# Up projections of a two-layer encoder: two blocks of seven products per group in place of one, their sums folded into the group's own accumulators, and the convolution done in two halves

## The chip, the core and the metric

The kernel runs on one core of one Trainium2 chip. The metric is device time in microseconds (us) of one execution of the whole program; the kernel before takes 2402.25 us, the median of three runs (2401.57 to 2403.32).

## The reference, cut to what matters

Two encoder layers over 256 tokens of width 2048, all in float32. Each layer is an attention mixer with a residual, and a gated feed-forward net (FFN) with a residual. The change is in the FFN:

```python
def conv_ffn(x, w_up, conv_w, conv_b, w_down):
    h = jnp.einsum("bsd,df->bsf", x, w_up)          # 2048 -> 2 * 5632
    g, u = h[..., :D_FF], h[..., D_FF:]
    gp = jnp.pad(g, ((0, 0), (1, 1), (0, 0)))
    g = conv_w[0] * gp[:, :-2] + conv_w[1] * gp[:, 1:-1] + conv_w[2] * gp[:, 2:] + conv_b
    return jnp.einsum("bsf,fd->bsd", jax.nn.gelu(g) * u, w_down)
```

Its input `x` is the RMS-normalised residual stream. In the kernel the normalising factor of each token is applied behind the product (`rstd`), the gain before it.

## The kernel before, in words

**A product.** TensorE computes in a float32 form of reduced mantissa. Each float32 operand is therefore split into a high part (a cast on ScalarE, L231) and a low part (a subtraction on VectorE, L234), and each product is three matmuls into the same PSUM bank: high by high, high by low, low by high (L195 to L197). The activations of the FFN (`yT`, 16 tiles of 128 features by 256 tokens) are split once per layer. The weights are streamed: `wunit` loads 128 x 1024 float32 values (512 KB: two tiles of 128 rows by 512 columns) into `raw`, a ring of 5 buffers, by a DMA from the SyncE queue, casts them into `wh` and subtracts into `wl`, rings of 4 buffers each. `a_unit` then issues 12 matmuls of 128 x 512 with it: two tiles of 128 features by two blocks of 128 tokens by three. A unit's buffers come free when its last matmul is done, so ScalarE and VectorE can be at most some three units ahead of TensorE.

**The up projections.** `up_group` (L835) makes one of 11 groups per layer: 512 columns of the gate side (x=0) and 512 of the up side (x=1), each 8 units long, in the four PSUM banks of the tag `gm`, one for each side and token block. Four more banks, tags `s` and `tp`, serve everything else. Units 0 to 3 of both sides alternate, then come units 4 to 7 of the gate side and 4 to 7 of the up side.

**The block of seven products.** For unit 3 (`UPK`), the 2 x 2 x 2 block of token blocks, feature tiles and sides is done by the Strassen-Winograd scheme: seven products (21 matmuls) in place of eight (24), with sums of the activations formed once per layer (`y_forms`, L330) and sums of the weights formed by four subtractions of 128 x 512 on VectorE (L951 to L955) beside their splits (`column_forms`, L936). `seven_products` (L966) adds three of the products straight into three `gm` banks and puts four into the extra banks. `extra_parts` (L840) turns these into four sums in SBUF with a ScalarE copy and four VectorE additions, `scaled_parts` (L852) multiplies each by `rstd` on ScalarE, and at the end of a side VectorE reads the bank, multiplies by `rstd` and adds the sum (L878, two per side). The down projections use the same scheme, which the change leaves alone.

**Behind a side.** VectorE transposes the side in blocks of 32 x 32 (L279), and 16 small DMAs (L273, 12 from GpSimdE's queue, 4 from SyncE's) move the blocks into `qk` tiles, so that features lie on partitions. `convolved` (L889) works on the gate side: per 128 features one ScalarE operation and two on VectorE (L897, L899), then one Gelu over all. `multiplied` (L925) makes the product of the two sides (L928), sometimes the sums for the down projection (`row_forms`), and splits it.

**What sets the order.** Each engine runs its instructions in order. The builder's scheduler places them; the code postpones work with `later(n, fn)`, which runs `fn` at the n-th next `tick()`. `tick` stands in `up_group` after each of the units 0 to 3 and after every second unit of each side, eight per group. The convolution is due two ticks after the end of the gate side, the multiplication two after the end of the group. `ffn` (L1031) runs groups 0 to 5, the down projections of their features, groups 6 to 10, and theirs; a half's down projections are two calls of `chunk_pair` (L1017).

Of the kernel before, what the change touches and what calls it, by code (L numbers as in the profile page):

```python
# [71 lines left out]
def trunk_kernel(ctx: ExitStack, tc, a, out):  # L72
    nc = tc.nc
# [12 lines left out]
    def nm(s):  # L86
        uid[0] += 1
        return f"{s}_{uid[0]}"
# [27 lines left out]
    def tps(tag, bufs):  # L116
        return psum.tile([P, 512], F32, name=nm(tag), tag=tag, bufs=bufs)
# [179 lines left out]
    def transposes(c, gain, res):  # L297
# [4 lines left out]
        for j in range(4):  # L302
            res[c * 4 + j] = y_tile(ps[j // 2][:, j % 2, :], gain, c * 4 + j)

    def turned_rows(c, gain, res):

        z = att.tile([P, 2, 512], F32, name=nm("z"), tag="sc", bufs=1)
        V.transpose(z, h[:, :, c * 512:(c + 1) * 512])
        pf = att.tile([P, 8, P], F32, name=nm("hT"), tag="pt", bufs=2)
        moved(z.rearrange("p t k -> p (t k)"), pf)  # L310

        def tiles():
            for j in range(4):
                res[c * 4 + j] = y_tile(pf.rearrange("p (t j) q -> p j t q", t=2)[:, j], gain, c * 4 + j)
            if res is formed.get("of") and c == UPK // 2:
                y_forms(pf.rearrange("p (t j) q -> p j t q", t=2), gain)
        return tiles

    formed = {}
# [7 lines left out]
        V.tensor_tensor(f[:, 3], a12, f[:, 1], op=ALU.subtract)  # L327
        return f

    def y_forms(src, gain):  # L330

        y = tmp.tile([P, 2, 2, P], F32, name=nm("yf"), tag="ry")
        for k in range(2):
            S.activation(y[:, k], src[:, UPK % 2 * 2 + k], AF.Copy, scale=gain[:, 2 * UPK + k:2 * UPK + k + 1])
        f = form_sums("scc", *(y[:, k, t] for k in range(2) for t in range(2)))
        form = []
        for x, tag in enumerate(("R", "Rq")):
            high = tmp.tile([P, 2, P], F32R, name=nm("form"), tag="t0")
            low = const.tile([P, 2, P], F32R, name=nm("form"), tag=tag, bufs=1)
            split(high, low, f[:, 2 * x:2 * x + 2])  # L340
            form += [(high[:, k], low[:, k]) for k in range(2)]
        formed["form"] = form
# [71 lines left out]
    def quad(slot, dtype=F32):  # L414
        return att.tile([P, 4, SEQ], dtype, name=nm("qk"), tag=f"qk{slot}", bufs=1)
# [226 lines left out]
    def new_sc():  # L642
        return att.tile([P, 2, 512], F32, name=nm("sc"), tag="sc", bufs=1)
# [188 lines left out]
    yT = mixer_out(a["ev_out"], mix, ln[:, 2, :])  # L832


    def up_group(layer, j, yT, rstd, prod, *more):  # L835

        sides, extra, sums = {}, [], []
        src = [a["up"][layer, j, x] for x in range(2)]

        def extra_parts():  # L840

            b1, b5, b6, b7 = extra
            s1, x0, x1, y1 = (tmp.tile([P, 512], F32, name=nm("sum"), tag=tag) for tag in ("rx", "ry", "ry", "rx"))
            S.copy(s1, b1)
            V.tensor_tensor(x0, s1, b6, op=ALU.add)
            V.tensor_tensor(x1, x0, b7, op=ALU.add)
            V.tensor_tensor(x0, x0, b5, op=ALU.add)  # L847
            V.tensor_tensor(y1, x1, b5, op=ALU.add)
            sums.extend([[s1, x1], [x0, y1]])
            later(1, scaled_parts)  # L850

        def scaled_parts():  # L852

            for x in range(2):
                for t in range(2):
                    S.activation(sums[x][t], sums[x][t], AF.Copy, scale=rstd[0][:, t:t + 1])  # L856

        pss = [[tps("gm", 4), tps("gm", 4)] for _ in range(2)]
        for u in range(4):
            if not j and u == 2:  # L860
                rstd.append(row_factor())
            if u == UPK:
                extra += [tps("s", 2), tps("tp", 2), tps("tp", 2), tps("s", 2)]
                seven_products(pss, extra, column_forms(src, u, True), u, yT, formed["form"], True, True)
                later(1, extra_parts)
            else:
                for x in range(2):
                    a_unit(pss[x], src[x], u, yT, KT)
            tick()
        for x in range(2):  # L870
            for u in range(4, 8):
                a_unit(pss[x], src[x], u, yT, KT)
                if u % 2 == 1:
                    tick()
            z = (tmp.tile([P, 8, P], F32, name=nm("z"), tag="z", bufs=1) if x else
                 new_sc().rearrange("p t (f k) -> p (t f) k", k=P))
            for t in range(2):
                out = V.scalar_tensor_tensor(z.rearrange("p (f t) k -> p t f k", t=2)[:, t],  # L878
                                       pss[x][t].rearrange("p (f k) -> p f k", k=P), rstd[0][:, t:t + 1],
                                       sums[x][t].rearrange("p (f k) -> p f k", k=P), op0=ALU.mult, op1=ALU.add)  # L880
                if t:
                    tc.keep_in_program_order(out)
# [6 lines left out]
    def convolved(layer, j, sides):  # L889

        g4, c4 = sides[0], quad(4)
        sides[2] = c4
        for i in range(4):
# [3 lines left out]
            V.scalar_tensor_tensor(c[:, 1:SEQ], g[:, 0:SEQ - 1], convw[:, layer, 0, f:f + 1],  # L897
                                   c[:, 1:SEQ], op0=ALU.mult, op1=ALU.add)
            V.scalar_tensor_tensor(c[:, 0:SEQ - 1], g[:, 1:SEQ], convw[:, layer, 2, f:f + 1],  # L899
                                   c[:, 0:SEQ - 1], op0=ALU.mult, op1=ALU.add)  # L900
        S.activation(c4, c4, AF.Gelu_apprx_tanh)

    def new_forms(g0, n):

# [109 lines left out]
            tick()  # L1014
        return pss

    def chunk_pair(src, c, act, forms, nk, done):  # L1017

        nu = nk // 2
        heads = nu - 3 if nu > 10 else nu - 2  # L1020
        pss = pair_head(src, c, act, forms, sorted(forms), heads, nk)
        if not c:
            flush()
        for x in range(2):
            for u in range(heads, nu):
                a_unit(pss[x], src[c + x], u, act, nk)
            if c:
                tick()
            done(pss[x], c + x)

    def ffn(layer, yT, gain, last=False):  # L1031
        rstd, res = [], None
        for g0, g1, seven in HALVES:
            prod, forms = [], {}
            for j in range(g0, g1):
                up_group(layer, j, yT, rstd, prod, forms, g0, seven)
            nk = 4 * (g1 - g0)
            src = [a["down"][layer, c, 2 * g0:2 * g1] for c in range(4)]
            if g0:
                res = [None] * KT  # L1040
                if last:
                    finish_all(src, prod, forms, nk)
                    return
            for c in (0, 2):
                chunk_pair(src, c, prod, forms, nk, lambda ps, x: finish_chunk(ps, x, gain, res, 1 + x if x < 2 else 1))
        return res

    yT = ffn(0, yT, ln[:, 1, :])
# [280 lines left out]
def _paired_up(w):  # L1329

    w = w.copy()
    x, y = w[:, :, 0, UPK].copy(), w[:, :, 1, UPK].copy()
    w[:, :, 0, UPK] = np.concatenate([x[..., :512], y[..., :512]], axis=-1)
    w[:, :, 1, UPK] = np.concatenate([y[..., 512:], x[..., 512:]], axis=-1)
    return w


# [69 lines left out]
```

## Time and profile before

| | |
|---|---|
| runs | 2402.25 us (median of 3; 2401.57 to 2403.32) |
| the profiled execution | 2402.49 us, of which the span from first to last instruction is 2400.6 us |
| mean granted TensorE clock | 0.999 |
| matmuls, VectorE instructions, ScalarE instructions | 10895, 2461, 1954 |
| HBM read | 458.48 MB, 192 GB/s over the span |

Times in the profile are from the span's start. PE is TensorE, PEld its weight loads, DVE VectorE, ACT ScalarE, POOL GpSimdE, SP SyncE. The matmuls of the two FFNs' up projections lie from about 640 to 920 us, 1080 to 1325, 1690 to 1965 and 2110 to 2320 us. A matmul's shown duration overlaps that of the next one, since they are pipelined; how far apart two starts are tells what one costs. VectorE's and ScalarE's shown durations overlap a little too.

### The profile page before, as it was taken

What the parts mean: (1) busy time and instruction counts of PE and PEld (TensorE: products, weight loads), DVE (VectorE), ACT (ScalarE), POOL (GpSimd) and SP (SyncE); (2) the same over time, 40 slices, a digit from 0 to 9 for tenths busy, and PEclk for the clock granted to TensorE, in tenths of its full rate; (3) what the DMA queues carried; (4) which work ended last, traced back from release to release, by engine and by line L of the source; (5) the groups of instructions that cost most, each with busy time, mean ns of one, the idle gap of its engine ahead of it and who ended that gap; (6) DMA issues with size and microseconds to landing.
All of it is one profiled execution on the core that took longest, in us unless ns stands there. A gap on an engine that the chain in (4) does not pass through costs nothing.

```text
span 2400.6 us, 32954 instructions
## 1 busy us (share of the span) xinstructions
PE 2386.9 (99%) x10895; PEld 1983.1 (83%) x10895; DVE 1859.8 (77%) x2461; ACT 1374.5 (57%) x1954; POOL 539.7 (22%) x940
## 2 busy tenths in 40 slices
PE   9999999999999999999999999999999999999998
PEld 7888888888888888888888888888888888888887
DVE  6576567676778898778989867676788887788887
ACT  7455455566556565445656657555565654456664
POOL 1142023322222422004232100422223320033220
PEclk9999999999999999999999999999999999999999
DMA  8778678766767877668777764667678876678874
GB/s 306 208 196 236 198 198 237 211 201 193 215 198 220 222 216 212 204 206 216 213 227 211 220 204 134 188 202 206 208 215 222 217 220 199 207 218 213 241 212 156
DMA packets 287531, 505.64 MB, mean 211 GB/s; under 512 B 159096, under 2 KB 160504, under 8 KB 287360
## 3 DMA queue, kind: packets, MB, share of 16 engines
q1 hardware_dynamic: 256848, 470.15, 64.1%
q0 software_dynamic: 30080, 32.74, 8.0%
q8 instruction: 85, 1.39, 0.2%
q14 instruction: 86, 0.70, 0.1%
q10 hardware_dynamic: 432, 0.66, 0.1%
HBM read 458.48 MB, written 2.18 MB: 192 GB/s over the span
## 4 chain that ended last, share of the span: by engine, by line
PE 59%; DVE 3%; DMA 2%; issue 1%; POOL 1%; ACT 1%; SPq 1%; DVEq 0%; ACTq 0%; POOLq 0%
PE gm L196 16%; PE gm L197 16%; PE gm L195 16%; PE gm L145 2%; DVE wl L234 1%; PE gm L978 1%; PE gm L979 1%; PE gm L977 1%; POOL qk L273 1%; PE gm L150 1%; DMA qk<-z 1%; PE tp L978 1%; PE tp L979 1%; PE tp L977 1%; PE s L978 1%
## 5 line engine op out<-in xcount | busy, mean ns | idle before, releaser
L231 ACT CAST wh<-raw 128x1024 fp32r<-128x1024 f32 (+1 forms) x897 | 936.1, 1048 | 811.5 <-PE gm L197 607.3
L234 DVE TENSOR_TENSOR wl<-raw,wh 128x1024 fp32r<-128x1024 f32 (+1 forms) x897 | 1083.3, 1215 | 383.7 <-ACT wh L231 373.0
L196 PE MATMUL gm<-wl,yT 128*128 128x512 f32 x2092 | 815.6, 390 | 2.3 <-DVE wl L234 2.2
L195 PE MATMUL gm<-wh,yT 128*128 128x512 f32 x2092 | 816.1, 390 | 0.0
L197 PE MATMUL gm<-wh,yT 128*128 128x512 f32 x2092 | 814.6, 389 | 0.0
L196 PEld LDWEIGHTS gm<-wl,yT 128*128 128x128 f32 x2092 | 392.9, 188 | 86.2 <-DVE wl L234 6.3
L197 PEld LDWEIGHTS gm<-wh,yT 128*128 128x128 f32 x2092 | 392.8, 188 | 81.8 <-DVE yT L240 0.2
L195 PEld LDWEIGHTS gm<-wh,yT 128*128 128x128 f32 x2092 | 392.8, 188 | 81.2 <-issue 0.4
L273 POOL DMA_DIRECT2D qk<-sc x264 | 152.2, 584 | 855.3 <-issue 358.4
L273 POOL DMA_DIRECT2D qk<-z x392 | 226.3, 585 | 257.1 <-DVE z L279 232.7
L196 PE MATMUL gm<-wl,prod 128*128 128x512 f32 x518 | 201.5, 389 | 0.0
L195 PE MATMUL gm<-wh,prod 128*128 128x512 f32 x518 | 201.5, 389 | 0.0
L197 PE MATMUL gm<-wh,prod 128*128 128x512 f32 x518 | 201.5, 389 | 0.0
L196 PEld LDWEIGHTS gm<-wl,prod 128*128 128x128 f32 x518 | 97.3, 188 | 20.2
L195 PEld LDWEIGHTS gm<-wh,prod 128*128 128x128 f32 x518 | 97.2, 188 | 20.2
L197 PEld LDWEIGHTS gm<-wh,prod 128*128 128x128 f32 x518 | 97.2, 188 | 20.2
L196 PE MATMUL gm<-wl,mix 128*128 128x512 f32 x256 | 100.1, 391 | 0.4 <-DVE wl L234 0.4
L195 PE MATMUL gm<-wh,mix 128*128 128x512 f32 x256 | 100.0, 391 | 0.0
L197 PE MATMUL gm<-wh,mix 128*128 128x512 f32 x256 | 99.6, 390 | 0.0
L273 POOL DMA_DIRECT2D hT<-z x72 | 41.5, 585 | 199.6 <-PE gm L197 75.4
L856 ACT ACTIVATE sum<-sum,rstd 128x512 f32<-128x512 f32 x88 | 58.9, 716 | 25.4 <-DVE sum L847 16.1
L145 PE MATMUL gm<-yT,wh 128*128 128x512 f32 x256 | 59.5, 390 | 0.0
(356 smaller groups left out, 2640.0 us busy)
## 6 DMA issues: line engine op xcount, KB each, us to landing
raw<-in_up SPq DMA_DIRECT2D x352, 512.0 KB, 4.5
raw<-in_down SPq DMA_DIRECT2D x176, 512.0 KB, 4.4
raw<-in_eva_qk SPq DMA_DIRECT2D x96, 512.0 KB, 4.4
raw<-in_eva_v SPq DMA_DIRECT2D x46, 512.0 KB, 6.0
raw<-in_evb_qk SPq DMA_DIRECT2D x32, 512.0 KB, 4.6
raw<-in_ev_out SPq DMA_DIRECT2D x32, 512.0 KB, 4.3
raw<-in_od_qk SPq DMA_DIRECT2D x32, 512.0 KB, 4.1
raw<-in_od_out SPq DMA_DIRECT2D x32, 512.0 KB, 4.1
```

Of the source, the lines that this page charges most:

```text
L145: T.matmul(ps.rearrange("p a b -> p (a b)"), wh[:, k * P:(k + 1) * P], act[u * 8 + k].rearrange("p a b -> p (a b)"), start=(u == 0 and k = ...
L150: T.matmul(ps[:, 1, :], wl[:, k * P:(k + 1) * P], act[u * 8 + k][:, 0, :], start=False, stop=(u * 8 + k == KT - 1))
L195: T.matmul(ps[t], ah, wh[:, sl], start=(kt == 0), stop=False)
L196: T.matmul(ps[t], ah, wl[:, sl], start=False, stop=False)
L197: T.matmul(ps[t], al, wh[:, sl], start=False, stop=(kt == nk - 1))
L231: first = S.copy(dst_h, src)
L234: V.tensor_tensor(dst_l, src, dst_h.bitcast(F32), op=ALU.subtract)
L273: (nc.sync if i in on_sync else G).dma_start(dst[j * 32:(j + 1) * 32, :, i * 32:(i + 1) * 32], z[i * 32:(i + 1) * 32].rearrange("p (b j c) ...
L856: S.activation(sums[x][t], sums[x][t], AF.Copy, scale=rstd[0][:, t:t + 1])
L977: T.matmul(ps, ah, wh, start=own and first, stop=False)
L978: T.matmul(ps, ah, wl, start=False, stop=False)
L979: T.matmul(ps, al, wh, start=False, stop=own and last)
```

## The change

- **Which units.** `UPK` becomes `(1, 3)`: units 1 and 3 are done by seven products each, in every group but a layer's first, which is done in full. The host's packing of the weights (`_paired_up`) follows.
- **The front.** The four products of a block that went into the extra banks are issued ahead, while the group before is still running (`up_front`): those of unit 1 ahead of the third unit from the end of its gate side, those of unit 3 ahead of the third from the end of its up side. For group 6 they stand in the second `chunk_pair` of the down projections. Both units' products add up in the same four banks.
- **The fold.** `merged` forms the Winograd sums inside these four banks (ScalarE copies into two of them, VectorE additions into two), and the banks then *are* the next group's accumulators. The groups take the banks `gm` and `s`/`tp` by turns.
- **The direct products.** The three products left of each block (`up_direct`) are added on top when the group starts. They need the other side's weight unit as it is, which is loaded a second time for that, and split. The form `t4` made in the front is kept till then.
- **The order of units.** A group does all units of the gate side (0, 2, 4 to 7), then all of the up side, with six ticks.
- **The end of a side.** ScalarE reads each bank and multiplies by `rstd` (two per side); `sums`, `scaled_parts` and L878 go. Both sides use one buffer `z`.
- **The convolution** is due in two halves, two and four ticks behind the gate side, each with a Gelu of its own; the multiplication three ticks behind the group.

```diff
-UPK = 3
+UPK = (1, 3)
...
+    def up_front(layer, j, yT):
+        gm = (j >= HALVES[0][1]) == j % 2
+        b1, b7, b6, b5 = (tps(*(("gm", 4) if gm else (tag, 2))) for tag in ("s", "s", "tp", "tp"))
+        direct = []
+        def block(n):
+            u = UPK[n]
+            w11, t1, t2, t3, t4 = front_forms([a["up"][layer, j, x] for x in range(2)], u, j)
+            s1, s2, s3, s4 = formed[u]
+            for ps, form, w in ((b1, token_block(yT, 2 * u, 0), w11), (b7, s3, t3), (b6, s2, t2), (b5, s1, t1)):
+                products(ps, form, w, n == 0, u == UPK[-1])
+            direct.append((u, s4, t4))
+        def merged():
+            s1, x0, x1 = (tmp.tile([P, 512], F32, name=nm("sum"), tag=tag) for tag in ("rx", "ry", "ry"))
+            S.copy(s1, b1)
+            V.tensor_tensor(x0, s1, b6, op=ALU.add)
+            V.tensor_tensor(x1, x0, b7, op=ALU.add)
+            V.tensor_tensor(b6, x0, b5, op=ALU.add)
+            S.copy(b7, x1)
+            V.tensor_tensor(b5, x1, b5, op=ALU.add)
+        block(0)
+        return [[b1, b7], [b6, b5]], direct, merged, block
...
+    def front_forms(src, u, home):
+        ra, rb = (wts.tile([P, UN], F32, name=nm("raw"), tag="raw", bufs=RAW) for _ in range(2))
+        nc.sync.dma_start(ra, src[0][u])
+        nc.sync.dma_start(rb, src[1][u])
+        w11, w12, w22, w21 = ra[:, 0:512], ra[:, 512:UN], rb[:, 0:512], rb[:, 512:UN]
+        t1 = tmp.tile([P, 512], F32, name=nm("t1"), tag="rx")
+        V.tensor_tensor(t1, w12, w11, op=ALU.subtract)
+        V.tensor_tensor(w12, w22, w12, op=ALU.subtract)
+        wa, wb = ([wts.tile([P, UN], F32R, name=nm(x), tag=x, bufs=4) for x in ("wh", "wl")] for _ in range(2))
+        split(*wa, ra)
+        V.tensor_tensor(w22, w22, t1, op=ALU.subtract)
+        split(*(x[:, 0:512] for x in wb), w22)
+        split(*(x[:, 512:UN] for x in wb), t1)
+        V.tensor_tensor(w21, w21, w22, op=ALU.subtract)
+        t4 = fourth(home, u)
+        split(*t4, w21)
...
+    def up_direct(pss, src, yT, u, s4, t4):
+        wh, wl = wunit(src[1][u])
+        products(pss[1][0], s4, [x[:, 0:512] for x in (wh, wl)], onto=True)
+        products(pss[0][0], token_block(yT, 2 * u + 1, 0), [x[:, 512:UN] for x in (wh, wl)], onto=True)
+        products(pss[0][1], token_block(yT, 2 * u + 1, 1), t4, onto=True)
...
+        for x in range(2):
+            for n, u in enumerate(units):
+                if not x and u == units[-3] and after:
+                    nxt = up_front(*after)
+                if x and nxt and u == units[-3]:
+                    nxt[3](1)
...
+                    own_unit(pss[x], src[x], u, yT, u == units[-1])
...
+            if x and nxt:
+                nxt[2]()
+            z = new_z("f k")
             for t in range(2):
-                out = V.scalar_tensor_tensor(z.rearrange("p (f t) k -> p t f k", t=2)[:, t],
-                                       pss[x][t].rearrange("p (f k) -> p f k", k=P), rstd[0][:, t:t + 1],
-                                       sums[x][t].rearrange("p (f k) -> p f k", k=P), op0=ALU.mult, op1=ALU.add)
+                S.activation(z.rearrange("p (f t) k -> p t f k", t=2)[:, t],
+                             pss[x][t].rearrange("p (f k) -> p f k", k=P), AF.Copy, scale=rstd[0][:, t:t + 1])
...
-                later(2, lambda: convolved(layer, j, sides))
-        later(2, lambda: multiplied(j, sides, prod, *more))
+                later(2, lambda: convolved(layer, j, sides, 0))
+                later(4, lambda: convolved(layer, j, sides, 1))
+        later(3, lambda: multiplied(j, sides, prod, *more))
```

Over the whole program TensorE issues 54 matmuls of 128 x 512 fewer (18 blocks more, three spared by each), VectorE 64 instructions more, ScalarE 124 more, and SyncE 40 loads of 512 KB more; GpSimdE's count is the same.

**VectorE at a block's forms.** Before, in the second group of a half: `t` and `raw` are the weight sums (L951 to L955), `wl` and `form` the low parts, `qk` the convolution.

```order
L951 TENSOR_TENSOR t_3218_16883<-raw_16879 128x512
L234 TENSOR_TENSOR wl_16842<-raw_16839,wh_16841 128x1024
L897 SCALAR_TENSOR_TENSOR qk_16707<-qk_16617,convw,qk_16707 128x255 x2
L899 SCALAR_TENSOR_TENSOR qk_16707<-qk_16617,convw,qk_16707 128x255 x2
L897 SCALAR_TENSOR_TENSOR qk_16707<-qk_16617,convw,qk_16707 128x255 x2
L899 SCALAR_TENSOR_TENSOR qk_16707<-qk_16617,convw,qk_16707 128x255 x2
L234 TENSOR_TENSOR wl_16860<-raw_16857,wh_16859 128x1024
L952 TENSOR_TENSOR raw_16879<-raw_16880,raw_16879 128x512
L234 TENSOR_TENSOR wl_16887<-raw_16880,wh_16886 128x1024
L234 TENSOR_TENSOR form_16897<-t_3218_16883,form_16896 128x512
L954 TENSOR_TENSOR raw_16880<-raw_16880,t_3218_16883 128x512
L234 TENSOR_TENSOR wl_16893<-raw_16879,wh_16892 128x1024
```

Now, on the gate side of a group, for the block of unit 1 of the next one (the sums are L894 to L901):

```order
L279 STREAM_TRANSPOSE z_16480<-z_16480 128x1024
L234 TENSOR_TENSOR wl_16552<-raw_16549,wh_16551 128x1024
L974 SCALAR_TENSOR_TENSOR qk_16427<-qk_16302,convw,qk_16427 128x255 x2
L234 TENSOR_TENSOR wl_16577<-raw_16574,wh_16576 128x1024
L894 TENSOR_TENSOR t_3142_16600<-raw_16596 128x512
L895 TENSOR_TENSOR raw_16596<-raw_16597,raw_16596 128x512
L898 TENSOR_TENSOR raw_16597<-raw_16597,t_3142_16600 128x512
L901 TENSOR_TENSOR raw_16597<-raw_16597 128x512
L234 TENSOR_TENSOR wl_16604<-raw_16596,wh_16603 128x1024
L234 TENSOR_TENSOR wl_16606<-raw_16597,wh_16605 128x512
L234 TENSOR_TENSOR wl_16606<-t_3142_16600,wh_16605 128x512
L234 TENSOR_TENSOR form_16615<-raw_16597,form_16615 128x512
```

The convolution no longer stands between a block's forms (its last two operations come ahead of them), and the block has one split of 128 x 1024 and three of 128 x 512 where it had three and one.

**VectorE at the end of a group.** Before, the four sums (L845 to L848) and the end of the gate side:

```order
L845 TENSOR_TENSOR sum_16926<-sum_16925,tp_16877 128x512
L234 TENSOR_TENSOR wl_16977<-raw_16974,wh_16976 128x1024
L846 TENSOR_TENSOR sum_16927<-sum_16926,s_16878 128x512
L234 TENSOR_TENSOR wl_16995<-raw_16992,wh_16994 128x1024
L847 TENSOR_TENSOR sum_16926<-sum_16926,tp_16876 128x512
L848 TENSOR_TENSOR sum_16928<-sum_16927,tp_16876 128x512
L234 TENSOR_TENSOR wl_17034<-raw_17031,wh_17033 128x1024
L234 TENSOR_TENSOR wl_17052<-raw_17049,wh_17051 128x1024
L234 TENSOR_TENSOR wl_17070<-raw_17067,wh_17069 128x1024
L878 SCALAR_TENSOR_TENSOR sc_17010<-gm_16742,rstd_15653,sum_16925 128x4x128
L878 SCALAR_TENSOR_TENSOR sc_17010<-gm_16743,rstd_15653,sum_16927 128x4x128
L279 STREAM_TRANSPOSE sc_17010<-sc_17010 128x1024
```

Now, on the up side: the fold (L862 to L866), the splits of the next group's two direct units (`wl_16914`, `wl_16929`) and of its unit 0, six of the eight convolution operations (L972, L974), and the transpose:

```order
L862 TENSOR_TENSOR sum_16882<-sum_16881,tp_16594 128x512
L234 TENSOR_TENSOR wl_16866<-raw_16863,wh_16865 128x1024
L863 TENSOR_TENSOR sum_16883<-sum_16882,s_16593 128x512
L864 TENSOR_TENSOR tp_16594<-sum_16882,tp_16595 128x512
L866 TENSOR_TENSOR tp_16595<-sum_16883,tp_16595 128x512
L234 TENSOR_TENSOR wl_16914<-raw_16911,wh_16913 128x1024
L972 SCALAR_TENSOR_TENSOR qk_16837<-qk_16712,convw,qk_16837 128x255 x2
L974 SCALAR_TENSOR_TENSOR qk_16837<-qk_16712,convw,qk_16837 128x255 x2
L234 TENSOR_TENSOR wl_16929<-raw_16926,wh_16928 128x1024
L234 TENSOR_TENSOR wl_16944<-raw_16941,wh_16943 128x1024
L972 SCALAR_TENSOR_TENSOR qk_16837<-qk_16712,convw,qk_16837 128x255 x2
L279 STREAM_TRANSPOSE z_16890<-z_16890 128x1024
```

The fold stands around the split of the side's last unit (`wl_16866`) and ahead of all that the next group needs; three splits of the next group stand ahead of the transpose, which waits for the end of the side, as three of the up side's stood before.

**TensorE at the start of a group.** Before, the last product of a group is followed by unit 0 of the gate and of the up side, in `gm` banks. Now the accumulators `s_16592`, `s_16593` and `tp_16594` were made by the front, and the direct products go onto them:

```order
L877 MATMUL gm_16197<-wh_16865,yT_15709 128x512
L877 MATMUL tp_16594<-wh_16913,form_15395 128x512
L877 MATMUL tp_16594<-wl_16914,form_15395 128x512
L877 MATMUL tp_16594<-wh_16913,form_15396 128x512
L877 MATMUL s_16592<-wh_16913,yT_15380 128x512
L877 MATMUL s_16592<-wl_16914,yT_15380 128x512
L877 MATMUL s_16592<-wh_16913,yT_15380 128x512
L877 MATMUL s_16593<-form_16615,yT_15380 128x512 x3
L877 MATMUL tp_16594<-wh_16928,form_15455 128x512
L877 MATMUL tp_16594<-wl_16929,form_15455 128x512
```

So the first matmul of a group now waits for the third VectorE addition of the fold (L864), and the seventh for ScalarE's copy behind the second.

More of the change, by code (lines that the diff above doesn't have):

```diff
@@ L870, in up_group, with token_block, products @@
[L870 to L873, printed above, removed]
+            V.tensor_tensor(b6, x0, b5, op=ALU.add)
[3 more added lines that the diff above has]
+        return [[b1, b7], [b6, b5]], direct, merged, block
+    def token_block(act, kt, t):
+        return [act[kt][:, x, t * P:(t + 1) * P] for x in range(2)]
+    def products(ps, form, w, first=False, last=False, onto=False):
+        (ah, al), (wh, wl) = form, w
+        for i, (x, y) in enumerate(((ah, wh), (ah, wl), (al, wh))):
+            T.matmul(ps, x, y, start=first and i == 0, stop=last and i == 2, skip_group_check=onto)
@@ new lines, in own_unit @@
+    def own_unit(ps, src, u, act, last):
+        wh, wl = wunit(src[u])
+        for t, k in [(t, k) for t in range(2) for k in range(2)] if last else [(t, k) for k in range(2) for t in range(2)]:
+            sl = slice(k * 512, (k + 1) * 512)
+            products(ps[t], token_block(act, 2 * u + k, t), [x[:, sl] for x in (wh, wl)], last=last and k == 1, onto=True)
+    def up_direct(pss, src, yT, u, s4, t4):
[3 more added lines that the diff above has]
+        products(pss[0][1], token_block(yT, 2 * u + 1, 1), t4, onto=True)
@@ new lines, in up_group @@
+    def up_group(layer, j, yT, rstd, prod, front, after, *more):
+        sides = {}
+        src = [a["up"][layer, j, x] for x in range(2)]
+        if front:
+            pss, direct = front[:2]
+            units = [u for u in range(8) if u not in UPK]
+            for u, s4, t4 in direct:
+                up_direct(pss, src, yT, u, s4, t4)
+        else:
+            pss = [[tps("gm", 4), tps("gm", 4)] for _ in range(2)]
+            units = list(range(8))
+        nxt = None
+        for x in range(2):
+            for n, u in enumerate(units):
+                if not j and not x and u == 2:
+                    rstd.append(row_factor())
+                if not x and u == units[-3] and after:
+                    nxt = up_front(*after)
+                if x and nxt and u == units[-3]:
+                    nxt[3](1)
+                if front:
+                    own_unit(pss[x], src[x], u, yT, u == units[-1])
+                else:
+                    a_unit(pss[x], src[x], u, yT, KT)
+                if n % 2 == 1 or n == len(units) - 1 and n % 2 == 0:
@@ L1015, in pair_head, with chunk_pair @@
         return pss
-    def chunk_pair(src, c, act, forms, nk, done):
+    def chunk_pair(src, c, act, forms, nk, done, after=None):
         nu = nk // 2
+        nxt = None
         heads = nu - 3 if nu > 10 else nu - 2
@@ L1025, in chunk_pair @@
             for u in range(heads, nu):
+                if not x and u == nu - 1 and after:
+                    nxt = up_front(*after)
+                if x and nxt and u == nu - 2:
+                    nxt[3](1)
                 a_unit(pss[x], src[c + x], u, act, nk)
+            if x and nxt:
+                nxt[2]()
             if c:
@@ L1035, in ffn @@
             for j in range(g0, g1):
-                up_group(layer, j, yT, rstd, prod, forms, g0, seven)
+                front = up_group(layer, j, yT, rstd, prod, front, j + 1 < g1 and (layer, j + 1, yT), forms, g0, seven)
             nk = 4 * (g1 - g0)
@@ L1044, in ffn @@
             for c in (0, 2):
-                chunk_pair(src, c, prod, forms, nk, lambda ps, x: finish_chunk(ps, x, gain, res, 1 + x if x < 2 else 1))
+                front = chunk_pair(src, c, prod, forms, nk,
+                                   lambda ps, x: finish_chunk(ps, x, gain, res, 1 + x if x < 2 else 1),
+                                   c and not g0 and (layer, g1, yT))
         return res
```

85 lines of the change are left out of this document (39 added, 46 removed).

## The prediction

> **What bounds the kernel now.** I read the page first, then the busy times by stretch, then TensorE's waits, then the timeline of one group. The page gives the span and the engines:
>
> ```profile
> span 2400.6 us, 32954 instructions
> PE 2386.9 (99%) x10895; PEld 1983.1 (83%) x10895; DVE 1859.8 (77%) x2461; ACT 1374.5 (57%) x1954; POOL 539.7 (22%) x940
> ```
>
> TensorE is busy for all but 13.7 us. An average over stages may hide a stage with another limit, so here are three stretches by engine (columns: stretch, its length, then busy us and count of PE, PEld, DVE, ACT, POOL, the granted clock, the DMA engines' busy share, GB/s): one period of an up group in layer 1, 40 us of up groups in layer 0, and 40 us of down projections.
>
> ```profile
> 1832.38:1875.78 43.40, 43.20 (x190) 35.41 (x189) 38.07 (x52) 26.58 (x36) 13.83 (x24) 1.00 0.81 222
> 1160.00:1200.00 40.00, 40.00 (x178) 33.09 (x177) 34.30 (x47) 24.59 (x32) 13.82 (x24) 1.00 0.75 209
> 1000.00:1040.00 40.00, 40.00 (x178) 33.07 (x177) 32.30 (x35) 20.05 (x21) 0.00 (x0) 1.00 0.70 220
> ```
>
> In the up groups too TensorE is the limit, at full clock; VectorE is second with 38.07 of 43.40 us (88%), ScalarE has over a third to spare. What TensorE waited for in the FFNs (us in total, times, longest), with two rows of the waits of the others in layer 1:
>
> ```profile
> PE gm L196 <- DVE wl L234: 2.5, 5, 0.9
> PE tp L978 <- DVE wl L234: 0.6, 1, 0.6
> ...
> ACT wh L231 <- PE gm L197: 196.7, 133, 3.6
> ...
> DVE t L951 <- DMA raw<-in_up: 5.6, 8, 1.2
> ```
>
> So it waited 3.1 us in all, each time for VectorE's low parts. The third row says why it is so little: ScalarE's casts wait for TensorE to give a buffer back, that is, weights are ready up to three units ahead. The up groups' own stalls lie where the reserve runs out, behind the block of seven products:
>
> ```profile
> 1824.90 0.39 PE L195 MATMUL gm<-wh,yT 128*128 128x512 f32 x1
> ...
> 1832.38 0.39 PE L977 MATMUL gm<-wh,yT 128*128 128x512 f32 x1
> ...
> 1837.21 0.39 PE L195 MATMUL gm<-wh,yT 128*128 128x512 f32 x1
> 1837.80 0.50 PE L196 MATMUL gm<-wl,yT 128*128 128x512 f32 x1 [0.20 <-DVE wl L234]
> 1838.13 0.40 PE L197 MATMUL gm<-wh,yT 128*128 128x512 f32 x1
> ...
> 1875.78 0.39 PE L977 MATMUL gm<-wh,yT 128*128 128x512 f32 x1
> ```
>
> From 1824.90 to 1832.38 there are 33 matmuls: 7.48 / 33 = 0.2267 us each, whatever the 0.39 us shown. The block's 21 take 1837.21 - 1832.38 = 4.83 us, 0.07 more than 21 x 0.2267. Then come 0.59 and 0.33 us where 0.227 each is usual: a stall of 0.36 and 0.10 of restart, 0.46 in all. 189 matmuls make the period: 42.84 + 0.07 + 0.46 = 43.37, measured 43.40.
>
> **The change, term by term.** *Matmuls removed.* A block spares three. Before there are 22 blocks (two layers by 11 groups), after 40 (two layers by 10 groups by two); 18 x 3 = 54 matmuls go, and since TensorE is the limit each is worth its distance: 54 x 0.2267 = **-12.2 us**. [...]
>
> *Slower products.* The 18 blocks more bring the block's excess of 0.07 us with them, **+1.3 us**. Products on a bank that another engine wrote are not in the trace; the nearest rows are these same ones, so I bound the term by 0 and 2.6 us (twice the excess) and keep 1.3.
>
> *VectorE per group.* Its rows, with starts that tell what one costs when they follow each other:
>
> ```profile
> 1859.17 1.40 DVE L878 SCALAR_TENSOR_TENSOR z<-gm,rstd,sum 128x512 f32<-128x512 f32 x2
> 1860.61 1.25 DVE L279 STREAM_TRANSPOSE z<-z 128x1024 f32<-128x1024 f32 x1
> 1861.78 1.19 DVE L234 TENSOR_TENSOR wl<-raw,wh 128x1024 fp32r<-128x1024 f32 x1
> ...
> 1865.15 0.87 DVE L897 SCALAR_TENSOR_TENSOR qk<-qk,convw,qk 128x255 f32<-128x255 f32 x2
> 1865.94 0.87 DVE L899 SCALAR_TENSOR_TENSOR qk<-qk,convw,qk 128x255 f32<-128x255 f32 x2
> ...
> 1869.45 0.68 DVE L952 TENSOR_TENSOR raw<-raw,raw 128x512 f32<-128x512 f32 x1
> 1870.05 1.22 DVE L234 TENSOR_TENSOR wl<-raw,wh 128x1024 fp32r<-128x1024 f32 x1
> 1871.19 0.68 DVE L234 TENSOR_TENSOR form<-t,form 128x512 fp32r<-128x512 f32 x1
> 1871.79 0.68 DVE L954 TENSOR_TENSOR raw<-raw,t 128x512 f32<-128x512 f32 x1
> ```
>
> A 512-wide subtraction or low part takes 0.60 us (1869.45 to 1870.05), a 1024-wide one 1.14, the two L878 1.44, a transpose 1.17, two convolution steps 0.79. Plain units stay at 14 (12 own, 2 direct). The old block is four subtractions, three wide low parts and one narrow; the two new ones have eight, two and six: +4 x 0.60 - 1.14 + 5 x 0.60 = +4.26. The four sums stay four. The four L878 go: -2.88. Net +1.4 us on 38.07, 39.5 us, while TensorE's share is 186 x 0.2267 + 0.14 = 42.3 us. VectorE goes from 88% to 93% of the group and isn't the limit. What matters then is whether its work comes in time.
>
> *ScalarE* loses four scalings per group and gains four bank reads, one Gelu call, a copy, and the narrower casts. For the reads the nearest row is the scaling; for the casts, the rows by group:
>
> ```profile
> L856 ACT ACTIVATE sum<-sum,rstd 128x512 f32<-128x512 f32 x88 | 58.9, 716 | 25.4 <-DVE sum L847 16.1 <-DVE sum L845 8.8 <-ACT wh L231 0.2
> L231 ACT CAST form<-t 128x512 fp32r<-128x512 f32 x37 | 22.8, 615 | 3.8 <-DVE t L951 3.8
> ```
>
> Reads for scalings cancel; five narrow casts more, one wide cast less, a copy and a call come to about 3.5 us on 26.58, some 30 of 42.3. It is hidden.
>
> *Where the reserve gets lowest.* Take the order of the instructions and the times above. At the end of the gate side ScalarE reads two banks (2 x 0.72, taken as 1.4 us) and VectorE transposes (1.17), with three splits already done ahead, 36 matmuls or 8.2 us. The front of unit 3 comes after those 36. VectorE then has one subtraction (0.6; two were done) and a wide split (1.14): ready at 1.4 + 1.17 + 1.74 = 4.3 us, needed at 8.2. The fold: its last bank is filled at 8.2 + 2.7 = 10.9 us, four additions are 2.4 and the copies on ScalarE perhaps 1, done by 14.5 at the latest; the direct products need it at the side's end, 84 x 0.2267 = 19.0 us. Margin 4.5. Up to there VectorE has the transpose, 0.60 + 1.14 + 3 x 0.60 of the forms, three splits, the fold, three splits ahead and six convolution steps: 1.17 + 3.54 + 3.42 + 2.40 + 3.42 + 2.37 = 16.3, with 1.4 of waiting 17.7 of 19.0. On the gate side TensorE does 18 direct, 72 plain and 12 front matmuls, 23.1 us. The front of unit 1 comes behind 18 + 36 of them, at 12.2 us; VectorE reaches its first operand after 1.4 + 1.17 + 0.79 + 2 x 1.14 + 4 x 0.60 + 1.14 = 9.2. Margin 3.0, the lowest of all. So in a steady group I see no stall, and the 3.1 us that the old burst of VectorE costs (convolution, block, multiplication and sums in one go) go for the most part: **-2.5 us** (bounds 0 and -3.7, the waits with six restarts of 0.1).
>
> *New waits.* At each layer's start and in front of group 6 the front falls beside other bursts (row sums, `h` additions), which the trace doesn't show together. Taking the longest wait shown, 0.9, for about one of these places: **+1.0 us** (0 to 9.2, see the first rival). Loads of weights: 18 units per group in place of 16. From the third stretch, 0.70 x 40 us for 220 GB/s x 40 us / 0.524 MB = 16.8 units, a unit is 1.67 us of all the DMA engines; two more per group raise the share from about 0.78 to 0.87. A load takes
>
> ```profile
> raw<-in_up SPq DMA_DIRECT2D x352, 512.0 KB, 4.5
> ```
>
> 4.5 us, and five buffers at 42.3 / 18 = 2.35 us apart leave 11.7, less what VectorE is ahead. I take it as hidden. The small moves keep their number and their queues; SyncE's four per side stand ahead of loads as before.
>
> *Sum*, against the profiled execution's 2402.49 us (its span is 2400.6; the median of the runs is 0.24 lower): -12.2 + 1.3 - 2.5 + 1.0 = -12.4 us, which gives **2390 us**.
>
> **The rivals.** *One stall per group remains.* The reserve runs out once in each of the 20 groups, say at the front of unit 1, at the old price of 0.46 us: 20 x 0.46 = 9.2 us, which replaces the term of +1.0 and the -2.5. Then 2402.5 - 12.2 + 1.3 + 9.2 - 3.1 = 2398 us. For it: VectorE at 93%, and 5.6 us in eight waits of its first subtraction for a load. Against: the margin of 3.0 us. Chance 0.15.
>
> *VectorE becomes the limit (slower).* Its work may not overlap as I counted. The multiplication, its splits, and the row sums that half of the groups have, are four kinds of rows (mean ns, or lowest, median and highest):
>
> ```profile
> L928 DVE TENSOR_TENSOR qk<-qk,qk 128x1024 f32<-128x1024 f32 x22 | 26.9, 1221 | 2.0 <-issue 1.1 <-DMA qk<-z 0.7
> L234 DVE TENSOR_TENSOR prod<-qk,prod 128x256 fp32r<-128x256 f32 x88 | 32.6, 417 | 0.0
> L324 DVE TENSOR_TENSOR sums<-qk x12: 282/284/289, 765.5 to 2261.9; 128x128 f32<-128x128 f32 x12
> L234 DVE TENSOR_TENSOR form<-sums,form 128x512 fp32r<-128x512 f32 x8 | 5.5, 683 | 0.0
> ```
>
> They make 1.22 + 4 x 0.42 + 4 x 0.28 + 0.68 = 4.7 us. If each instruction kept its whole shown duration, a group would have 14 + 2 wide low parts at 1.22, eight subtractions, six narrow low parts and four sums at 0.68, two transposes at 1.25, eight convolution steps at 0.48 (0.87 less half of 0.79) and these 4.7: 19.5 + 12.2 + 2.5 + 3.8 + 4.7 = 42.7 us, and with one wait of 1.4 for the banks 44.1, against TensorE's 42.3. In 20 groups 1.8 us each: 2390 + 36 = 2426 us. It decides from the point where VectorE needs over 40.9 us per group. The rows above speak against it: a start follows 0.60 us after one that lasts 0.68. [...] Chance 0.06.
>
> *The loads become late (slower).* At a DMA share of 0.87 a load may wait in line; if each of the 40 fronts gets its two tiles so late that the margin of 3.0 us is used up and TensorE waits the 0.7 us (5.6 / 8) that VectorE's first subtraction waits now, that is 28 us: 2418 us. Against: a share of 0.81 in the first stretch, without a wait of TensorE's that names a load. Chance 0.05.
>
> *It doesn't spare the matmuls:* excluded, the new order has 54 fewer.
>
> **How the numbers follow.** A measurement of this kernel can tell about 0.2%, 4.8 us, from no change. The forecast, all stalls together under some 4 us, has 0.74 and lies wholly on the faster side; the first rival, 0.15, is spread about 2398, half of it past 2397.4; the other two have 0.11 and are slower. Faster 0.81, same 0.08, slower 0.11. Low end: all old stalls gone with their restarts, no new ones and no slower products, 2402.5 - 12.2 - 3.7 = 2386.6; I take 2386. High end: the first rival with the slower products doubled, 2399.5; 2400. That leaves out the two slow rivals and a little more.
>
> **What would show it.** Right: 10841 matmuls recorded or so, the distance between starts still 0.227, the period of a group 42.3 us, VectorE at some 39.5 us of it, no wait of TensorE for a low part in most groups, none for the fold's additions. Wrong: a wait of TensorE that comes back once per group at the first front or the first direct product (first rival), TensorE gaps with VectorE full (second), or VectorE's first subtraction waiting for a load in every group by over 2 us (third).

## The result and the profile after

The changed kernel takes 2421.43 us (median of 4 runs, 2420.19 to 2426.92), the kernel before beside it 2401.91 (2399.75 to 2403.32): a ratio of 1.0086, 95% interval 1.0069 to 1.0104. It is slower by some 19.5 us where 12 us less were forecast. The first two lines of the page after:

```profile
span 2419.6 us, 33368 instructions
PE 2386.3 (99%) x10841; PEld 1974.4 (82%) x10841; DVE 1874.3 (77%) x2525; ACT 1409.4 (58%) x2078; POOL 537.4 (22%) x940
```

The 54 matmuls are gone, but TensorE is idle for 33.3 us (before 13.7) and no less busy (why is told below). The steady groups look as forecast (busy times by stretch: 40 us of layer 0, then one period in layer 1):

```profile
1160.00:1200.00 40.00, 40.00 (x177) 33.04 (x176) 37.82 (x55) 26.44 (x39) 13.78 (x24) 1.00 0.81 239
1851.82:1894.13 42.31, 42.31 (x187) 34.92 (x186) 38.72 (x55) 27.92 (x40) 13.79 (x24) 1.00 0.84 249
```

TensorE is full, the period is 42.31 us, VectorE has 38.72 of it, the DMA share is 0.84. Most of the loss lies elsewhere. From the starts of matmuls in the timeline, these are the stretches' lengths in us. (After the change, the first and third stretch of down projections also hold the fronts of group 6, 24 matmuls or 5.4 us each, and the first of its direct products, 3 matmuls or 0.7 us. The ranges given ahead for the up projections are off in part: before, they run from 660.7 to 920.3, 1047.8 to 1262.5, 1686.2 to 1945.3 and 2071.9 to 2287.6 us.)

| stretch | before | after |
|---|---|---|
| layer 0: up, first half | 259.60 | 260.18 |
| down, first half | 127.52 | 137.41 |
| up, second half | 214.72 | 205.31 |
| down, second half | 105.38 | 110.12 |
| attention, and layer 1: up, first half | 577.39 | 576.94 |
| down, first half | 126.64 | 139.33 |
| up, second half | 215.66 | 209.31 |
| down, second half | 105.48 | 112.34 |

Less the two fronts, the down projections, which the change leaves alone, lose 4.5 + 4.7 + 7.3 + 6.9 = 23.4 us (22.0 less the direct products too). Who waits for whom (us in total, times, longest):

```profile
DVE qk L972 <- ACT qk L971: 61.8, 20, 7.4
ACT qk L971 <- DMA qk<-z: 57.8, 20, 8.0
...
DVE qk L1004 <- DMA qk<-z: 18.7, 10, 4.3
...
PE gm L196 <- DVE wl L234: 11.6, 10, 1.8
...
PE tp L877 <- DVE wl L234: 4.7, 5, 1.5
...
PE gm L195 <- ACT wh L231: 2.8, 2, 1.9
```

TensorE waits for splits. But the engines that make them wait far longer for the small moves behind a side: ScalarE at the convolution's first operation (L971), VectorE at its second (L972) and at the multiplication (L1004). The last group of layer 1's first half shows how that reaches TensorE. First ScalarE's timeline, then VectorE's, GpSimdE's and TensorE's:

```profile
1937.15 1.25 ACT L953 ACTIVATE z<-s,rstd 128x512 f32<-128x512 f32 x2
1938.30 3.18 ACT L231 CAST wh<-raw 128x1024 fp32r<-128x1024 f32 x3
1943.14 1.05 ACT L231 CAST wh<-raw 128x1024 fp32r<-128x1024 f32 x1 [1.67 <-PE tp L877]
1945.86 1.05 ACT L231 CAST wh<-raw 128x1024 fp32r<-128x1024 f32 x1 [1.66 <-PE tp L877]
1954.01 2.08 ACT L971 ACTIVATE qk<-qk,convb,convw 128x256 f32<-128x256 f32 x4 [7.10 <-DMA raw<-in_down]
```

```profile
1933.70 1.23 DVE L1004 TENSOR_TENSOR qk<-qk,qk 128x1024 f32<-128x1024 f32 x1 [4.28 <-DMA qk<-z]
...
1938.45 1.24 DVE L279 STREAM_TRANSPOSE z<-z 128x1024 f32<-128x1024 f32 x1
...
1946.95 1.23 DVE L234 TENSOR_TENSOR wl<-raw,wh 128x1024 fp32r<-128x1024 f32 x1 [1.49 <-ACT wh L231]
1954.65 0.48 DVE L972 SCALAR_TENSOR_TENSOR qk<-qk,convw,qk 128x255 f32<-128x255 f32 x1 [6.47 <-ACT qk L971]
```

```profile
1939.99 6.88 POOL L273 DMA_DIRECT2D qk<-z  x12 [12.73 <-DVE z L279]
```

```profile
1956.32 0.39 PE L197 MATMUL gm<-wh,prod 128*128 128x512 f32 x1
1957.65 0.50 PE L195 MATMUL gm<-wh,prod 128*128 128x512 f32 x1 [0.95 <-ACT wh L231]
1959.81 0.50 PE L196 MATMUL gm<-wl,prod 128*128 128x512 f32 x1 [1.66 <-DVE wl L234]
```

The gate side is turned at 1938.45, and the convolution, which needs all of it moved, starts 15.6 us later. After five splits the convolution stands at the head of both queues; nothing behind it starts for 7.10 and 6.47 us, the reserve of three units runs out, and TensorE stands twice. (The row names a load; but the last of the moves, issued at 1946.29, took 7.4 us to land, to 1953.7, 0.3 us ahead of the start, and in the other three last groups the row names a move.) VectorE's first row is as telling: before that it had stood 4.28 us at the multiplication of the *group before*, so that this gate side was read late, at 1937.15, its two banks back to back without a wait for TensorE.

In these rows ScalarE keeps to the order of its queue: the load of the next cast was issued at 1942.48 and landed 4.9 us later, at 1947.4, and TensorE had been giving a buffer back every 2.72 us (1943.14, 1945.86), the next by some 1948.6 at that pace; still the cast starts only at 1956.57, behind the convolution, and VectorE's split of the same weights at 1958.54. One late operand held back a cast and a split whose load had landed.

### The profile page after: what moved, and what is told of

It is laid out like the page before. It is cut to its first block, busy times and chain, and to the rows that moved or that the text cites. A ratio compares the mean times of both kernels' runs of the same rounds, so it can differ in the third digit from the quotient of the medians.

```text
span 2419.6 us, 33368 instructions
## 1 busy us (share of the span) xinstructions
PE 2386.3 (99%) x10841; PEld 1974.4 (82%) x10841; DVE 1874.3 (77%) x2525; ACT 1409.4 (58%) x2078; POOL 537.4 (22%) x940
## 4 chain that ended last, share of the span: by engine, by line
PE 65%; DMA 12%; DVE 11%; issue 4%; POOL 4%; ACT 2%; SPq 2%; DVEq 0%; ACTq 0%; POOLq 0%
PE gm L196 14%; PE gm L195 14%; PE gm L197 14%; DMA qk<-z 9%; PE gm L877 5%; DVE wl L234 5%; PE s L877 4%; POOL qk L273 4%; PE tp L877 3%; PE gm L145 2%; DMA raw<-in_up 2%; SPq L273 2%; DVE z L279 1%; PE gm L150 1%; DVE qk L972 1%
## 5 line engine op out<-in xcount | busy, mean ns | idle before, releaser
L273 POOL DMA_DIRECT2D qk<-z x656 | 377.3, 583 | 1129.4 <-DVE z L279 1079.9
L196 PE MATMUL gm<-wl,yT 128*128 128x512 f32 x988 | 385.5, 390 | 1.6 <-DVE wl L234 1.6
L195 PE MATMUL gm<-wh,yT 128*128 128x512 f32 x988 | 386.7, 392 | 0.0
L197 PE MATMUL gm<-wh,yT 128*128 128x512 f32 x988 | 385.3, 390 | 0.0
L877 PE MATMUL gm<-wh,yT 128*128 128x512 f32 x832 | 265.8, 390 | 0.0
L877 PE MATMUL s<-wh,yT 128*128 128x512 f32 x672 | 218.5, 390 | 0.0
L196 PEld LDWEIGHTS gm<-wl,yT 128*128 128x128 f32 x988 | 185.7, 188 | 39.9 <-DVE wl L234 2.7
L197 PEld LDWEIGHTS gm<-wh,yT 128*128 128x128 f32 x988 | 185.5, 188 | 39.0 <-DVE yT L240 0.2
L195 PEld LDWEIGHTS gm<-wh,yT 128*128 128x128 f32 x988 | 185.6, 188 | 37.8 <-issue 0.4
L877 PEld LDWEIGHTS gm<-wh,yT 128*128 128x128 f32 x832 | 156.2, 188 | 32.9
L877 PE MATMUL tp<-wh,yT 128*128 128x512 f32 x576 | 180.6, 389 | 0.0
L877 PE MATMUL gm<-wl,yT 128*128 128x512 f32 x416 | 162.6, 391 | 0.7 <-DVE wl L234 0.7
L877 PEld LDWEIGHTS s<-wh,yT 128*128 128x128 f32 x672 | 126.2, 188 | 26.7
L877 PE MATMUL s<-wl,yT 128*128 128x512 f32 x336 | 131.4, 391 | 0.0
L877 PEld LDWEIGHTS tp<-wh,yT 128*128 128x128 f32 x576 | 108.1, 188 | 22.4
```

The lines of the kernel that those rows point to most:

```text
L195: T.matmul(ps[t], ah, wh[:, sl], start=(kt == 0), stop=False)
L196: T.matmul(ps[t], ah, wl[:, sl], start=False, stop=False)
L197: T.matmul(ps[t], al, wh[:, sl], start=False, stop=(kt == nk - 1))
L273: (nc.sync if i in on_sync else G).dma_start(dst[j * 32:(j + 1) * 32, :, i * 32:(i + 1) * 32], z[i * 32:(i + 1) * 32].rearrange("p (b j c) ...
L877: T.matmul(ps, x, y, start=first and i == 0, stop=last and i == 2, skip_group_check=onto)
```

## The experiments

All change only where the convolution stands, but for the last two, which say so. Held means that both halves are issued behind the reading of the up side's banks, ScalarE's part of it in a fixed order; which groups are held is one condition:

```diff
-            if not x:
+            held = not after              # the first experiment
+            if not x and not held:
                 later(2, lambda: convolved(layer, j, sides, 0))
                 later(4, lambda: convolved(layer, j, sides, 1))
+            if x and held:
+                convolved(layer, j, sides, 0, True)
+                convolved(layer, j, sides, 1, True)
...
-            S.activation(c, g, AF.Identity, ...)
+            ins = S.activation(c, g, AF.Identity, ...)
+            if pin:
+                tc.keep_in_program_order(ins)
```

**The last groups** (`held = not after`).

> The changed kernel, but in the last group of each half (four places) both halves of the convolution are issued after the up side's evacuation, in a fixed order, where the old kernel had them. Theory (a block at the head of ScalarE's and VectorE's queues): in the last group no front stands between the gate side's transposition and the convolution, so ScalarE reaches it before its 16 small moves have landed, both engines stand, and TensorE runs out of weights. From the stage times the four passages into the down projections cost 4.5 + 4.7 + 7.3 + 6.9 = 23.4 us more than before; so about 2421 - 23 = 2398 us, 2402 if some of the block's stalls stay. Rival 1 (VectorE has too much work around the end of a half, wherever the convolution stands): under 5 us come back, 2417 or more. Rival 2 (the lower clock after the stalls is the loss by itself, from something else): only the 9 us of half-clock products or nothing change.

Measured: 2413.57 us (ratio to the kernel before 1.0047, 1.0033 to 1.0062). 8 us came back, not 23. That lies between the theory's 2398 and rival 1's 2417: the theory had not seen that the last group begins late.

**The first groups** (`held = not j`).

> The changed kernel, but in the first group of each layer (two places) both halves of the convolution are issued after the up side's evacuation, in a fixed order; the last groups are left as they are. Theory: the 2.3 us of TensorE's stalls in layer 0 and 3.0 us in layer 1 around the second front of group 1 come from the same block at the head of the queues; about 2421 - 5 = 2416 us. Rival 1 (the first front and its forms are simply too much for VectorE beside a plain group): no change, 2421, the stalls stay at the second front.

Measured: 2414.64 us (1.0048, 1.0035 to 1.0061), 6.8 us less, near the theory. The stalls around the second front of group 1 are gone in both layers.

**Both** (`held = not after or not j`).

> Both: the convolution held back in the first group of a layer and in the last group of each half, the steady groups as in the changed kernel. Theory: the two add, 2421 - 23 - 5 = 2393 us, within 4 us of the 2390 that were predicted, and faster than the old kernel by about 9 us. Rival 1: 2412 or more.

Measured: 2402.16 us (1.0000, 0.9991 to 1.0009). Together they give 19.3 us, more than the 7.9 and 6.8 apart, but 9 us less than the theory.

**All groups** (`held = True`).

> The convolution held back in every group, undivided in time, behind the up side's evacuation, as the old kernel had it; fronts, fold and everything else as in the changed kernel. Theory: in a steady group the block's forms already stand between the transposition and the convolution, so holding it saves no stall there, but the burst (eight convolution steps, 3.2 us) then falls on the margin of 3.0 us in front of unit 1's block: 0 to 0.5 us of stall in each of 18 groups, 2393 to 2402 us. Rival (the steady groups lose time to the early convolution too): faster than the run with only first and last groups held, 2390 or less.

Measured: 2389.14 us (2388.54 to 2389.33; ratio 0.9943, 0.9931 to 0.9956). The rival was right: the steady groups cost 13 us as well, and the margin of 3.0 us bears the undivided convolution. Its page, then the two waits that are left of those above, and ScalarE at the last group shown before (the convolution is L975 there, the multiplication L1010):

```profile
span 2387.3 us, 33336 instructions
PE 2374.3 (99%) x10841; PEld 1973.5 (83%) x10841; DVE 1874.7 (79%) x2525; ACT 1422.4 (60%) x2078; POOL 538.9 (23%) x940
```

```profile
PE gm L196 <- DVE wl L234: 3.0, 3, 1.6
...
DVE qk L1010 <- DMA qk<-z: 1.3, 1, 1.3
```

```profile
1919.95 0.69 ACT L953 ACTIVATE z<-s,rstd 128x512 f32<-128x512 f32 x1 [0.40 <-PE s L877]
...
1936.28 0.69 ACT L953 ACTIVATE z<-tp,rstd 128x512 f32<-128x512 f32 x1 [0.67 <-PE tp L877]
1936.86 1.08 ACT L975 ACTIVATE qk<-qk,convb,convw 128x256 f32<-128x256 f32 x2
```

The same work (VectorE 1874.7 us, before the edit 1874.3; as many loads) takes 32 us less. The gate side's second bank is now read as soon as TensorE is done with it, and the convolution starts without waiting.

**The steady groups alone** (`held = after and j`).

> The convolution held behind the up side's evacuation only in the steady groups (neither a layer's first nor a half's last); the first and last groups as in the changed kernel. Theory, widened after the run with all groups held gave 2389 us and the one with first and last held 2402: in every group the early convolution stands at the head of ScalarE's and VectorE's queues until its moves have landed; in steady groups the weights made ahead cover the wait, but the lag is handed on to the next transposition, move and convolution. So the steady groups alone should give back more than the 13 us between those two runs: 2421 - 13 = 2408 us at most, 2400 if much of what stands in the last groups is handed-on lag. Rival (only the last and first groups lose time): 2416 or more.

Measured: 2401.76 us (1.0001, 0.9991 to 1.0010), 19.7 us less. Its stretches tell more: the four of down projections shrink from 137.4 + 110.1 + 139.3 + 112.3 = 499.2 to 134.9 + 106.6 + 134.5 + 109.0 = 484.9 us, although nothing in the last groups was changed. Most of what seemed to be theirs came from the groups ahead of them.

**The last two groups of each half** (`held = not after or j in (4, 9)`).

> The changed kernel with the convolution held behind the up side's evacuation in the last two groups of each half (eight groups of 22). Theory (lag handed on): a group whose convolution waited turns its up side late, so the next group's multiplication stands at VectorE's head for the moves, and its own gate side is turned late; the last group, which has the shortest up side, pays. Holding the last alone gave 2413.6 us; with the one before it held as well the last group starts without lag and the four passages into the down projections fall to about what the run with all held has: 2413.6 less 8 to 12, 2402 to 2406 us. Rival (the lag builds up over many groups, or each early convolution costs its own share): 22 groups share the 24 us between 2413.6 and 2389, so four more held give 4 to 5 us, 2409 us.

Measured: 2400.70 us (0.9990, 0.9981 to 1.0000). Four groups more give 12.9 us, above even the theory's 8 to 12. In its profile the stretches of down projections are 133.7, 104.9, 132.9 and 105.5 us, those of the run with all held 135.0, 104.9, 132.9 and 105.5. So, as far as the down projections go, holding the last two groups is enough: the lag that counts comes from the group before the last. The 11.6 us that are left against the run with all held are the price of the 14 groups whose convolution is still early.

**Held, in two halves** (`held = True`; the second half one tick later).

> The convolution held in every group as in the run with all held, but in two halves: the first behind the up side's evacuation, the second one tick later. Theory: what counts is that it stands behind the landing, not that it is whole or halved: 2389 us, within 3. Rival (dividing it is the loss): 2395 or more.

Measured: 2391.66 us (0.9962, 0.9949 to 0.9975). Dividing it isn't the loss. The 2.5 us above the run with all held (the two intervals overlap) can't be put down to dividing: in the last group of each half the order came out otherwise than the edit meant. There ScalarE has the first half ahead of the reading of the up side's banks, and the wait for the moves is back, once in each of the four groups:

```profile
ACT qk L975 <- DMA qk<-z: 11.6, 4, 4.1
```

**Early, but without the wait.** The convolution reads the residual tile `h`, and ScalarE's part of it is fixed in its order, as in the held runs; the rest is the changed kernel:

```diff
-            g, c = g4[:, i, :], c4[:, i, :]
-            S.activation(c, g, AF.Identity, ...)
+            g, c = h[:, 0, i * SEQ:(i + 1) * SEQ], c4[:, i, :]
+            tc.keep_in_program_order(
+                S.activation(c, g, AF.Identity, ...))
```

> The changed kernel with its early convolution, but the convolution reads the residual tile h, which lies ready, in place of the gate side's turned tile (the moves are still made, nobody reads them; so the output is not the reference's). In the order the convolution stands even a few splits earlier than in the changed kernel. Theory (the wait for the moves is the loss, not the place of the work): no wait left, 2389 to 2394 us. Rival (the work itself falls at a bad place, ahead of the fold and the splits): 2410 or more.

Measured: 2396.59 us (0.9974, 0.9965 to 0.9984). 25 of the 32 us come back with the convolution earlier than ever: it starts 4 us behind the gate side's transposition on average (14.5 in the changed kernel), and no wait stands ahead of it. So it is the wait. The fixed order alone doesn't remove it: in the last groups of the run in two halves ScalarE had that order and waited all the same. The remaining 7.5 us lie in the down projections (its stretches of them are 8.1 us longer than with all held), where another wait at VectorE's head grows, that of the first subtraction of a down projection's block for its load. First this run, then the one with all held:

```profile
DVE t L1028 <- DMA raw<-in_down: 26.1, 17, 3.8
```

```profile
DVE t L1033 <- DMA raw<-in_down: 17.2, 18, 2.4
```

That this is the cause was not tried.

**One block in place of two** (`held = True`, `UPK = (1,)`, the calls for the second block left out).

> The run with all convolutions held, but with one block of seven products per group (unit 1 only; unit 3 as a plain unit): 60 matmuls more, 20 blocks' excess fewer, 20 groups without the second burst of forms. Theory (the saving is the matmuls): 2389.1 + 60 x 0.2267 - 20 x 0.07 = 2401 us. Rival (the gain of the run with all held comes from VectorE's relief or from ScalarE's evacuation, not from the second block): 2392 or less.

Measured: 2405.69 us (1.0015, 1.0006 to 1.0024), 16.5 us above the run with both blocks, and 4.7 above the theory. The saving is mostly the matmuls: 60 x 0.2267 = 13.6 us of the 14.6 by which the spans of the profiled executions differ (2401.9 and 2387.3), or of the 16.5 between the medians. My 1.4 us for slower products don't show; what makes up the rest stays open.

## Why the prediction was wrong

Most of the sum held. There are 10841 matmuls. With the convolution held the period is 42.3 us with VectorE at 39.29 and ScalarE at 28.55 of it:

```profile
1794.49:1836.80 42.31, 42.31 (x187) 34.91 (x186) 39.29 (x55) 28.55 (x40) 13.83 (x24) 1.00 0.86 250
```

The forecast was 42.3, 39.5 and some 30, a DMA share of 0.87 (0.86 here), and a sum of -12.4 us; the profiled execution of this version took 2389.05, that is -13.4 against 2402.49. So the removed matmuls, VectorE's budget, the front's and the fold's margins and the loads held: no TensorE wait for a low part is left in that version's up groups. That the sum came within 1.0 us is luck in part. The -2.5 takes all of 3.1 us of old waits for the up groups' own, but two of the six, 1.2 us, lie in the attention mixer and one, 0.6 us, in the down projections (941.00):

```profile
1530.94 0.50 PE L196 MATMUL gm<-wl,yT 128*128 128x512 f32 x1 [0.87 <-DVE wl L234]
...
1603.62 0.50 PE L196 MATMUL gm<-wl,mix 128*128 128x512 f32 x1 [0.37 <-DVE wl L234]
```

Only 1.3 us in three waits could go. The matmuls make up 12.2 of the 13.4 us; how the rest divides, slower products included, isn't shown. None of the three rivals happened: no stall in each group, VectorE not the limit (it is as busy in the fast version as in the slow one), no loads at the fronts that TensorE waited for (VectorE's first subtraction waits for one in 18 of the 40 fronts, 21.3 us in all, and TensorE has no wait there).

The step that failed is "New waits ... +1.0 us (0 to 9.2)". It measured about 32 us, the difference between the changed kernel and the one with the convolution held. The error sits one step ahead of it, in "Where the reserve gets lowest": there six convolution steps were put into the up side's 19.0 us as work that can run when its turn comes, and the small moves were dismissed because they "keep their number and their queues". What changed was how soon their result is asked for. Two rows of the trace of before, which the prediction did not use, held the warning (ScalarE's waits at the convolution):

```profile
ACT qk L896 <- DMA qk<-sc: 12.9, 16, 1.8
...
ACT qk L896 <- DMA qk<-z: 4.7, 3, 1.8
```

In 19 of 22 groups the old convolution already waited for its moves, (12.9 + 4.7) / 19 = 0.9 us on average: it stood right at the landing. In the last group of layer 0's first half that is 15.5 us after the transposition (VectorE's row, then ScalarE's):

```profile
910.57 1.25 DVE L279 STREAM_TRANSPOSE sc<-sc 128x1024 f32<-128x1024 f32 x1
```

```profile
926.07 1.10 ACT L896 ACTIVATE qk<-qk,convb,convw 128x256 f32<-128x256 f32 x2 [1.83 <-DMA qk<-sc]
```

The ticks hide what changed. The convolution was due two ticks behind the gate side before as well, but these were the 48 matmuls of the rest of the up side, and it stood behind the up side's transposition in all 22 groups (in the prediction's rows 1860.61, then L897 at 1865.15). Now the up side is 72 matmuls long or more, two ticks end 48 to 60 matmuls (10.9 to 13.6 us) into it, and the convolution stands ahead of its transposition in all 22 groups. It starts no earlier for that: 14.5 us behind the gate side's transposition on average, before and after. Whoever asks earlier waits longer: all 22 wait, 57.8 us in 20 waits that name a move and 11.7 in two that name a load.

Nor did I follow a wait past its own group. In a steady group the weights made ahead cover it (TensorE stays full), so the reserve argument looked right there; but the up side is then read late, its moves leave late, and the next group's multiplication stands at VectorE's head (18.7 us in 10 waits) in front of the next gate side's transposition. The last group of a half has no front between its transposition and its convolution, 72 matmuls (16.3 us) in place of 84 on its up side, and the block of the down projections behind it; there the lag comes due. I had worked out the margins for a steady group only, and looked for new waits at the layers' starts and in front of group 6, not at the ends of halves.

Two pairs of TensorE's stalls also cost more than their length. The busy times around the stalls at the end and behind those at 1957.65 and 1959.81 (granted clock in the third column from the right):

```profile
2300.00:2309.00 9.00, 5.84 (x25) 4.29 (x23) 4.75 (x10) 5.41 (x10) 0.00 (x0) 0.97 0.48 145
2309.30:2315.30 6.00, 5.92 (x14) 4.67 (x15) 5.76 (x7) 3.78 (x5) 4.53 (x8) 0.50 0.68 144
1960.30:1963.70 3.40, 3.40 (x10) 2.63 (x9) 3.40 (x5) 2.40 (x3) 2.49 (x5) 0.50 0.77 187
```

For 6 and 3.4 us the clock is 0.50, and matmuls start 0.43 us apart in place of 0.227: about 24 x 0.2 = 4.8 us more. The 54 matmuls less would leave 2386.9 - 12.2 = 2374.7 us of TensorE's busy time, and the run with all held has 2374.3; the changed kernel has 11.6 more. Part of the rest is the stalls themselves: a matmul is shown with 0.39 us where 0.227 pass to the next start, so the first 0.16 us of a stall count as busy. How the rest divides beyond that isn't worked out.

## What to carry to other kernels

When an operation is moved ahead in an in-order queue, ask when its operand lands, not only whether its engine has time: a wait that the trace shows at its old place, however short, says that the operand lands no sooner. Here it landed as late as before (the convolution started 14.5 us behind the transposition on average, before and after), so the wait grew with every microsecond by which the operation was reached earlier, and everything behind it waited too. Work out the margins for the first and the last pass of a loop as well, where what stands between producer and consumer is missing. A reserve hides a wait, but not the lag that the wait hands on; look for the place where it comes due.

## What the runs showed of the hardware that was not expected

The clock fell after short stalls, and not each time. Two waits of 1.87 and 1.66 us with one matmul between them went with the 0.50 at the end. In the run with the first groups held, waits of 0.82 and 1.76 us near 940 us were followed by 3.2 us at 0.50:

```profile
944.40:947.60 3.20, 3.20 (x9) 2.52 (x8) 3.20 (x4) 1.81 (x4) 0.00 (x0) 0.50 0.61 189
```

In the changed kernel waits of 0.73 and 1.75 us at the same place were followed by full clock:

```profile
946.50:950.00 3.50, 3.50 (x15) 2.89 (x16) 3.50 (x7) 3.50 (x5) 0.00 (x0) 1.00 0.64 159
```

So like stalls had unlike ends; no run here shows why.
